# Inverse roots of the two recurrent mixers by one GpSimd power, in a two-block network on one Trainium2 core

## Chip, cores and metric

The program runs on one core of a Trainium2 chip. The metric is device time in microseconds (us) of one execution; three runs of the kernel before gave 1481.28 to 1483.36, median 1481.92. All data are float32, and all work from the input `x` to the output is in one launch.

## The reference, cut to what matters

The network has a first block of two attention layers and a second block of two layers, each `FFN, mixer, FFN`, with 256 tokens of width 1024. The change touches the mixer only. Its recurrent half (eight heads of 64) and its retention half (four heads of 128) are:

```python
kk = heads(k * k_k)
kk = kk * lax.rsqrt(jnp.maximum(jnp.sum(kk * kk, axis=-1, keepdims=True), 1e-24))
...
y = rwkv7_scan(r_h, heads(decay), k_h, v_h, -kk, kk * a_h)
mean = jnp.mean(y, axis=-1, keepdims=True)
var = jnp.mean(jnp.square(y - mean), axis=-1, keepdims=True)
y = ((y - mean) * lax.rsqrt(var + LN_X_EPS) * ln_w + ln_b)
...
o = retention_chunkwise(q, k, v)
o = o * lax.rsqrt(jnp.mean(o * o, axis=-1, keepdims=True) + NORM_EPS)
```

Three inverse roots per head and token, then: of the keys, of the recurrence's output, and of the retention's output. The mixer also has low-rank products (`w_lora_up`, `a_lora_up`) that make the decay and the factor `a`.

## The kernel before

Activations are kept transposed: 128 partitions of features, 256 tokens along the free axis. A weight tile comes from HBM (`raw`, four buffers), is split by ScalarE into a rounded high part (`whi`, line 115) and by VectorE into the rest (`wlo`, line 116), and each product is three matmuls (lines 129 to 131). `fetch_to` runs these loads four tiles ahead of their use.

In `mix` the eight recurrent heads are worked on in two units `b` of four. For each unit: `project` makes k, r and v (`proj_t`, then `shifted`, whose tile `pz` has two buffers in a ring); `operands` takes the norm of the keys; `chunks` makes the Gram matrices of four chunks of 64 tokens (`gram`, line 980) and inverts a triangular matrix by five doubling steps (tiles `t` and `dx`, line 963); `chain` runs the recurrence over the chunks and normalises its output. Then come `retention` and the output product. The functions are generators; the order in which an engine gets their instructions is chosen by a scheduler when the program is built, and each engine runs its own list strictly in that order. So the projections of unit 1 (`mm`) stand in TensorE's list between the small matmuls of unit 0.

One norm goes this way. `by_head` sums squares on TensorE into a PSUM tile `sums` (line 900), 128 tokens by 8 values. `rsqrt` (line 165) takes the inverse root on VectorE in twelve instructions: one for scale and offset, or for the floor (`ra`, line 172 or 174), two for a first guess by integer arithmetic (lines 175 and 176), and three Newton steps of three (lines 178 to 180). `spread2` (line 884) copies the eight values out to 64 columns each on ScalarE (`wide`, line 887, in the ring of `pz`) and transposes that on TensorE (`spread`, line 891), so that the factor stands beside the features. In `operands` a further matmul sums the bonus (`bonus`, line 945). The retention's root (line 1220) goes to TensorE without `wide`.

`lora_pair` (line 867) makes the low-rank products `pw` and `pa` and takes them through ScalarE as `sw` and `av`. For unit 1 it uses the PSUM banks of the projections (tag `mm`, line 1121).

Of the kernel before, what the change touches and what calls it, by code (L numbers as in the profile page):

```python
# [9 lines left out]
F32 = mybir.dt.float32  # L10
# [3 lines left out]
OP = mybir.AluOpType  # L14
# [37 lines left out]
class Net:  # L52
# [3 lines left out]
    def __init__(self, ctx, tc, plan, wstream, x, vec, vcols, ident):  # L56
        self.tc, self.nc = tc, tc.nc
        nc = self.nc
        self.wstream, self.plan = wstream, plan
        self.offs = {}  # L60
        off = 0
        for key, n in plan:
            self.offs[key] = (off, n)
            off += 128 * n
        self.order = [k for k, _ in plan]
        self.pos = {k: i for i, k in enumerate(self.order)}
        self.keep = ctx.enter_context(tc.tile_pool(name="keep", bufs=1))
        self.ring = ctx.enter_context(tc.tile_pool(name="ring", bufs=1))
        self.banks = Banks(ctx.enter_context(tc.tile_pool(name="banks", bufs=1, space=bass.MemoryType.PSUM)))
        xs = [self.keep.tile([128, 2, S], F32, name=f"x{i}") for i in range(4)]  # L70
        self.xs = xs
        self.x = [xs[k // 2][:, k % 2] for k in range(KT)]
        self.gain0 = self.keep.tile([128, KT], F32, name="gain0")
        self.vec = self.keep.tile([128, vec.shape[1]], F32, name="vec")
        nc.sync.dma_start(xs[0], x[:, 0:2])
        nc.scalar.dma_start(self.gain0, vec[:, vcols["norm0"]:vcols["norm0"] + KT])
        self.vcols = vcols
        self.ones = self.keep.tile([128, 128], F32, name="ones")
        nc.gpsimd.memset(self.ones, 1.0)
        self.ident = self.keep.tile([128, 128], F32, name="ident")  # L80
        nc.gpsimd.dma_start(self.ident, ident)
        self.ready = {}
        self.y = {}
        self.next = 0
        self.loads = {}
        self.between = lambda: None

        for i in range(1, 4):
            self.fetch_to(LEAD[i - 1])
            nc.sync.dma_start(xs[i], x[:, 2 * i:2 * i + 2])  # L90
        self.fetch_to(LEAD[3])
        nc.sync.dma_start(self.vec, vec)
# [68 lines left out]
            nc.scalar.activation(t, self.xs[i], AF.Square)  # L161
            nc.vector.tensor_tensor(sq, sq, t, op=OP.add)

    def rsqrt(self, src, shape, scale, eps, name, floor=None):

        nc = self.nc
        full = {"k": [128, 16], "q": [128, 2, 4], "m": [128, 2]}[name]
        a, y, t = (self.ring.tile(full, F32, tag=i + name, name=i, bufs=2)[..., :shape[-1]]
                   for i in ("ra", "ry", "rt"))
        v = nc.vector  # L170
        if floor is None:
            v.tensor_scalar(a, src, scale, eps, op0=OP.mult, op1=OP.add)
        else:
            v.tensor_scalar(a, src, floor, None, op0=OP.max)
        v.tensor_scalar(y.bitcast(I32), a.bitcast(I32), 1, None, op0=OP.logical_shift_right)
        v.tensor_scalar(y.bitcast(I32), y.bitcast(I32), -1.0, float(0x5f3759df), op0=OP.mult, op1=OP.add)
        for _ in range(3):
            v.tensor_tensor(t, y, y, op=OP.mult)
            v.scalar_tensor_tensor(t, t, -0.5, a, op0=OP.mult, op1=OP.mult)
            v.scalar_tensor_tensor(y, t, 1.5, y, op0=OP.add, op1=OP.mult)  # L180
        return y
# [642 lines left out]
    def mix(self, tag, l, cst):  # L824


        nc, tc, ident = self.nc, self.tc, self.ident
# [3 lines left out]
        with ExitStack() as c:  # L831
# [49 lines left out]
                    nc.scalar.activation(t, t, AF.Copy, scale=0.5, bias=0.5)  # L881
                q.update(sw=sw, av=av)

            def spread2(rn, tag):

                wide = work.tile([128, 2, 4, 64], F32, tag="pz", name="wide", bufs=2)
                nc.scalar.copy(wide, rn[:, :, :, None].to_broadcast([128, 2, 4, 64]))
                ps = psum.tile([128, 2, S], F32, tag=tag, name="spread")
                for u in range(2):
                    for tt in range(2):  # L890
                        nc.tensor.transpose(ps[:, u, tt * 128:tt * 128 + 128],
                                            wide[:, tt, 2 * u:2 * u + 2].rearrange("p e d -> p (e d)"), ident)
                return ps
# [19 lines left out]
            def operands(q, b):  # L913

                k, r, v, s_, a = (q[n] for n in ("k", "r", "v", "sw", "av"))
                ls, em = two("op1", "lsem")
                kk, kq = two("op2", "kkq")
                for u in range(2):
                    nc.vector.tensor_tensor_scan(ls[:, u], scan, s_[:, u], 0.0, op0=OP.mult, op1=OP.add)

                e1 = work.tile([128, 8, C + 1], F32, tag="e1", name="e1")
                nc.gpsimd.memset(e1[:, :, 0:1], 1.0)
                nc.scalar.activation(e1[:, :, 1:], c8(ls), AF.Exp, scale=DK)
                ec = work.tile([128, 2, 4], F32, tag="ec", name="ec", bufs=2)
                nc.scalar.copy(ec, e1[:, :, C].rearrange("p (u c) -> p u c", u=2))
                nc.scalar.activation(em, ls, AF.Exp, scale=-DK)
                for u in range(2):
                    nc.scalar.activation(kk[:, u], k[:, u], AF.Copy, scale=self.v(f"kk{l}", 2 * b + u))
                nc.scalar.activation(kq, kk, AF.Square)
                yield  # L930
                rn = self.rsqrt(by_head(kq, "inv"), [128, 2, 4], 1.0, 0.0, "q", floor=1e-24)
                kh = work.tile([128, 2, S], F32, tag="kh", name="kh")
                for u in range(2):
                    nc.scalar.activation(kh[:, u], a[:, u], AF.Identity, scale=self.v(f"ka{l}", 2 * b + u),
                                         bias=rest[:, 14 + 2 * b + u:15 + 2 * b + u])
                nc.vector.tensor_tensor(kh, kh, k, op=OP.mult)

                for u in range(2):
                    nc.vector.scalar_tensor_tensor(kq[:, u], r[:, u], self.v(f"rk{l}", 2 * b + u), kh[:, u],
                                                   op0=OP.mult, op1=OP.mult)  # L940
                yield
                sp = spread2(rn, "inv")
                nc.vector.tensor_tensor(kk, kk, sp, op=OP.mult)
                ps = psum.tile([128, 2, S], F32, tag="inv", name="bonus")
                nc.tensor.matmul(ps, blk, kq, start=True, stop=True)

                ar, bk = w8("ar", 128), w8("bk", 128)
                nc.vector.scalar_tensor_tensor(ar[:, :, 0:64], c8(kk), -1.0, e1[:, :, 0:C], op0=OP.mult, op1=OP.mult)
                nc.vector.tensor_tensor(a, kk, a, op=OP.mult)
                nc.vector.tensor_tensor(bk[:, :, 0:64], c8(a), c8(em), op=OP.mult)  # L950
                nc.vector.tensor_tensor(bk[:, :, 64:128], c8(kh), c8(em), op=OP.mult)
                nc.vector.tensor_tensor(ar[:, :, 64:128], c8(r), e1[:, :, 1:], op=OP.mult)
                bonus = work.tile([128, 2, S], F32, tag="bonus", name="bonus", bufs=2)
                nc.vector.tensor_tensor(bonus, ps, v, op=OP.mult)
                for u in range(2):
                    nc.scalar.activation(bonus[:, u], bonus[:, u], AF.Identity, bias=self.v(f"lb{l}", 2 * b + u))
                q.update(ec=ec, bonus=bonus, ar=ar, bk=bk)
# [77 lines left out]
            def chain(q, b):  # L1035
# [55 lines left out]
                y2 = w8("t1", 64, 1).rearrange("p (u c) t -> p u (c t)", u=2)  # L1091
                nc.scalar.activation(y2, y, AF.Square)
                yield
                rn = self.rsqrt(by_head(y2, "ch"), [128, 2, 4], 1.0 / 64, 64e-5, "q")
                yield
                sp = spread2(rn, "ch")
                nc.vector.tensor_tensor(y, y, sp, op=OP.mult)
                for u in range(2):
                    nc.vector.scalar_tensor_tensor(y[:, u], y[:, u], self.v(f"lw{l}", 2 * b + u), q["bonus"][:, u],
# [16 lines left out]
            def project(name, b):  # L1116
                q = units[b]
                mid = None
                if name == "v":
                    if b:  # L1120
                        lora_pair(q, 1, "mm")
                    else:
                        mid = lambda: lora_pair(q, 0, "inv")
                ps = led["kr".index(name) + 1] if b == 0 and name in "kr" else self.proj_t(psum, (tag, name, b), mid=mid)
                q[name] = work.tile([128, 2, S], F32, tag="p" + name, name="p" + name, bufs=2 if name == "v" else 1)
                shifted(ps, q[name], {"r": 0, "k": 4, "v": 8}[name] + 2 * b)
# [14 lines left out]
    def retention(self, tag, l, psum, work, cst, units):  # L1141
# [75 lines left out]
            if h:  # L1217
                norms(h - 1, sq[h - 1])
        norms(3, sq[3])
        rn = self.rsqrt(ps2, [128, 2, 4], 1.0 / 128, 1e-6, "q")  # L1220
        for h in range(4):
            sp = self.spread(psum, lambda tt: rn[:, tt, h:h + 1].to_broadcast([128, 128]))
            nc.vector.tensor_tensor(o[h], o[h], sp, op=OP.mult)
# [282 lines left out]
```

## Time and profile before

| | value |
|---|---|
| profiled execution, its own time | 1481.24 us |
| its span, first to last instruction | 1479.4 us |
| median of three runs | 1481.92 us |
| TensorE busy (matmuls) | 1442.0 us, 97% |
| VectorE busy | 1027.2 us, 69% |
| ScalarE busy | 739.7 us, 50% |
| GpSimd busy | 6.3 us in 43 instructions |
| mean granted TensorE clock | 0.988 |

TensorE is busy nearly all the time, in 1442.0 of 1479.4 us, so what can be won lies in its holes and in the stretches where its granted clock is below 1. Clock 1.00 means 2.4 GHz and 0.50 means 1.2 GHz. The two mixers begin near 522 us and 1097 us.

### The profile page before, as it was taken

The page shows a single profiled execution, that of the slowest core. Times are in us where ns is not written, and L with a number is a line of the kernel's source. Part 1 is how long each engine was busy: PE and PEld are TensorE (multiplying, and loading weights), DVE is VectorE, ACT ScalarE, POOL GpSimd, SP SyncE. Part 2 cuts the span into 40 slices and gives each one's busy share as a digit, 9 for nine tenths or more (in the row PEclk, how much of TensorE's full clock was granted, in tenths as well). Part 3 has the DMA queues.
Part 4 walks back from the last instruction along what each step waited for, and adds up shares of the span by engine and source line. Part 5 has one row for each costly group of instructions (what it writes and reads, how often), then busy time and mean ns, then how long its engine had stood idle before and what let it go on. Part 6 is the DMA issues. An engine that isn't in the chain of part 4 may idle for free.

```text
span 1479.4 us, 31824 instructions
## 1 busy us (share of the span) xinstructions
PE 1442.0 (97%) x13326; PEld 1379.1 (93%) x13326; DVE 1027.2 (69%) x1914; ACT 739.7 (50%) x1268; POOL 6.3 (0%) x43
## 2 busy tenths in 40 slices
PE   8899989999999989999999999999998999999997
PEld 7799979899999988899999999999997889999997
DVE  7879788976565676768655558556577757865564
ACT  6947555855444574235544445444466314554443
POOL 0000000000000000000000000000000000000000
PEclk9999999999999998999999999999999999999998
DMA  8234534265555541124555555555552213555561
GB/s 291 79 129 143 174 121 136 86 219 174 185 185 184 161 165 64 50 84 139 173 186 182 182 181 176 180 184 186 185 172 86 73 45 101 169 177 183 185 185 44
DMA packets 63601, 222.01 MB, mean 150 GB/s; under 512 B 7745, under 2 KB 9025, under 8 KB 63457
## 3 DMA queue, kind: packets, MB, share of 16 engines
q1 hardware_dynamic: 62928, 219.31, 46.3%
q8 instruction: 104, 1.70, 0.5%
q10 hardware_dynamic: 432, 0.53, 0.1%
q14 instruction: 41, 0.33, 0.1%
q0 software_dynamic: 96, 0.13, 0.0%
HBM read 218.90 MB, written 1.05 MB: 149 GB/s over the span
## 4 chain that ended last, share of the span: by engine, by line
PE 89%; DVE 4%; ACT 4%; issue 1%; DMA 1%; SPq 0%; DVEq 0%; ACTq 0%
PE gu L129 11%; PE gu L130 11%; PE gu L131 11%; PE mm L130 6%; PE mm L129 6%; PE acc L129 6%; PE acc L130 6%; PE acc L131 6%; PE mm L131 6%; PE dx L963 1%; DVE wlo L116 1%; ACT whi L115 1%; PE t L963 1%; PE gu L271 1%; PE gram L980 1%
## 5 line engine op out<-in xcount | busy, mean ns | idle before, releaser
L115 ACT CAST whi<-raw 128x1024 fp32r<-128x1024 f32 (+1 forms) x412 | 426.6, 1038 | 441.7 <-PE gu L130 161.4
L116 DVE TENSOR_TENSOR wlo<-raw,whi 128x1024 fp32r<-128x1024 f32 (+1 forms) x412 | 499.4, 1213 | 205.6 <-ACT whi L115 205.1
L129 PE MATMUL gu<-hh,whi 128*128 128x256 f32 x1344 | 381.2, 284 | 0.0
L130 PE MATMUL gu<-hl,whi 128*128 128x256 f32 x1344 | 380.7, 283 | 0.0
L131 PE MATMUL gu<-hh,wlo 128*128 128x256 f32 x1344 | 380.5, 283 | 0.0
L129 PEld LDWEIGHTS gu<-hh,whi 128*128 128x128 f32 x1344 | 258.0, 192 | 0.6 <-issue 0.4
L130 PEld LDWEIGHTS gu<-hl,whi 128*128 128x128 f32 x1344 | 258.1, 192 | 0.0
L131 PEld LDWEIGHTS gu<-hh,wlo 128*128 128x128 f32 x1344 | 258.0, 192 | 0.0
L131 PE MATMUL acc<-mh,wlo 128*128 128x256 f32 x704 | 198.8, 283 | 0.0
L130 PE MATMUL acc<-ml,whi 128*128 128x256 f32 x704 | 198.8, 283 | 0.0
L129 PE MATMUL acc<-mh,whi 128*128 128x256 f32 x704 | 197.7, 284 | 0.1
L129 PE MATMUL mm<-hh,whi 128*128 128x256 f32 x608 | 180.4, 297 | 8.8 <-ACT whi L115 6.7
L130 PE MATMUL mm<-hl,whi 128*128 128x256 f32 x608 | 177.1, 291 | 0.1
L131 PE MATMUL mm<-hh,wlo 128*128 128x256 f32 x608 | 175.6, 289 | 0.0
L130 PEld LDWEIGHTS acc<-ml,whi 128*128 128x128 f32 x704 | 135.2, 192 | 0.0
L131 PEld LDWEIGHTS acc<-mh,wlo 128*128 128x128 f32 x704 | 135.2, 192 | 0.0
L129 PEld LDWEIGHTS acc<-mh,whi 128*128 128x128 f32 x704 | 134.3, 192 | 0.8 <-issue 0.4
L129 PEld LDWEIGHTS mm<-hh,whi 128*128 128x128 f32 x608 | 117.8, 194 | 15.4 <-ACT whi L115 6.7
L130 PEld LDWEIGHTS mm<-hl,whi 128*128 128x128 f32 x608 | 117.8, 194 | 3.7 <-issue 2.0
L131 PEld LDWEIGHTS mm<-hh,wlo 128*128 128x128 f32 x608 | 117.9, 194 | 1.2 <-DVE wlo L116 0.2
L246 DVE TENSOR_TENSOR t<-gu,rs 128x512 f32<-128x512 f32 x88 | 60.5, 691 | 55.1 <-PE gu L131 55.1
L137 ACT CAST mh<-g 128x256 fp32r<-128x256 f32 x88 | 35.4, 406 | 100.6 <-DVE g L249 100.6
(392 smaller groups left out, 2205.9 us busy)
## 6 DMA issues: line engine op xcount, KB each, us to landing
raw<-in_stream SPq DMA_DIRECT2D x404, 512.0 KB, 3.5
raw<-in_stream SPq DMA_DIRECT2D x4, 280.0 KB, 2.7
x<-in_x SPq DMA_DIRECT2D x4, 256.0 KB, 5.1
raw<-in_stream SPq DMA_DIRECT2D x4, 256.0 KB, 5.3
lora<-in_lora SPq DMA_DIRECT2D x2, 512.0 KB, 6.1
dec<-in_dec SPq DMA_DIRECT2D x1, 512.0 KB, 5.5
out<-o SPq DMA_DIRECT2D x2, 256.0 KB, 3.0
out<-o ACTq DMA_DIRECT2D x2, 256.0 KB, 2.9
```

The costliest lines, as they stand in the source:

```text
L115: nc.scalar.copy(hi, raw)
L116: nc.vector.tensor_tensor(lo, raw, hi.bitcast(F32), op=OP.subtract)
L129: mm(out, ah, bh, start=start, stop=False, skip_group_check=True)
L130: mm(out, ah, bl, start=False, stop=False, skip_group_check=True)
L131: mm(out, al, bh, start=False, stop=stop, skip_group_check=True)
L137: nc.scalar.copy(hi, src)
L246: nc.vector.tensor_tensor(t, ps, self.rsb, op=OP.mult)
L271: mm(ps[:, u], part, self.h[k][0], start=(i + j == 0), stop=False, skip_group_check=True)
L963: nc.tensor.matmul(ps[p, n], lhs(e, p, n), rhs(e, p, n), start=True, stop=True)
L980: nc.tensor.matmul(ps[p, n], bk[p, 4 * u + n, w], ar[p, 4 * u + n], start=True, stop=True)
```

## The change

A new `power` takes the place of `rsqrt` at three places: the keys' norm, the recurrence's norm, and the retention's norm. It has one VectorE instruction for scale or floor (`rp`) and one GpSimd `tensor_tensor` that raises it to the power -0.5 (`rr`). The first block and the RMS norms go on with `rsqrt`. `wide` moves from the ring of `pz` to the two tiles that otherwise hold the squares (`sqt` for unit 0, `sqa` for unit 1). The second `lora_pair` writes to the banks `ch` of the recurrence in place of `mm`.

```diff
+        self.mhalf = self.keep.tile([128, 2, 4], F32, name="mhalf")
+        nc.gpsimd.memset(self.mhalf, -0.5)
...
+    def power(self, src, scale, eps, floor=None):
+
+        nc = self.nc
+        n = src.shape[-1]
+        a, y = (self.ring.tile([128, 2, 4], F32, tag=i, name=i, bufs=2)[..., :n] for i in ("rp", "rr"))
+        if floor is None:
+            nc.vector.tensor_scalar(a, src, scale, eps, op0=OP.mult, op1=OP.add)
+        else:
+            nc.vector.tensor_scalar(a, src, floor, None, op0=OP.max)
+        nc.gpsimd.tensor_tensor(y, a, self.mhalf[..., :n], op=OP.pow)
+        return y
...
-            def spread2(rn, tag):
-
-                wide = work.tile([128, 2, 4, 64], F32, tag="pz", name="wide", bufs=2)
+            def spread2(rn, b, tag):
+
+
+                wide = self.ring.tile([128, 2, 4, 64], F32, tag=("sqt", "sqa")[b], name="wide")
...
-                rn = self.rsqrt(by_head(kq, "inv"), [128, 2, 4], 1.0, 0.0, "q", floor=1e-24)
+                rn = self.power(by_head(kq, "inv"), None, None, floor=1e-24)
...
-                sp = spread2(rn, "inv")
+                sp = spread2(rn, b, "inv")
...
-                rn = self.rsqrt(by_head(y2, "ch"), [128, 2, 4], 1.0 / 64, 64e-5, "q")
+                rn = self.power(by_head(y2, "ch"), 1.0 / 64, 64e-5)
                 yield
-                sp = spread2(rn, "ch")
+                sp = spread2(rn, b, "ch")
...
-                        lora_pair(q, 1, "mm")
+                        lora_pair(q, 1, "ch")
...
-        rn = self.rsqrt(ps2, [128, 2, 4], 1.0 / 128, 1e-6, "q")
+        rn = self.power(ps2, 1.0 / 128, 1e-6)
```

The scheduler builds another order from this. The first place is VectorE's list in the first mixer, from the keys' sums of unit 0 to the factor's use. Before, from the ninth of the twelve root instructions on, the end of the second Newton step (names: `kkq` holds the keys and their squares, `bonus` the bonus sums, `pz` and `pk` the shifted projection of unit 1):

```order
L180 SCALAR_TENSOR_TENSOR ry<-rt,ry 128x8
L116 TENSOR_TENSOR wlo<-raw,whi 128x1024
L178 TENSOR_TENSOR rt<-ry 128x8
L116 TENSOR_TENSOR wlo<-raw,whi 128x1024
L179 SCALAR_TENSOR_TENSOR rt<-rt,ra 128x8
L116 TENSOR_TENSOR wlo<-raw,whi 128x1024
L180 SCALAR_TENSOR_TENSOR ry<-rt,ry 128x8
L852 TENSOR_TENSOR pz<-mm,rs 128x2x256
L943 TENSOR_TENSOR kkq<-kkq,spread 128x512
```

Of the change, from the sums on:

```order
L174 TENSOR_SCALAR rp<-sums 128x8
L948 TENSOR_TENSOR kh<-kh,pk 128x512
L863 TENSOR_TENSOR pz<-mm,rs 128x2x256
L951 SCALAR_TENSOR_TENSOR kkq<-pr,vec,kh 128x256 x2
L963 TENSOR_TENSOR bk<-kh,lsem 128x8x64
L955 TENSOR_TENSOR kkq<-kkq,spread 128x512
L966 TENSOR_TENSOR bonus<-bonus,pv 128x512
L960 SCALAR_TENSOR_TENSOR ar<-kkq,e_6789 128x8x64
L961 TENSOR_TENSOR av<-kkq,av 128x512
L118 TENSOR_TENSOR wlo<-raw,whi 128x1024
L962 TENSOR_TENSOR bk<-av,lsem 128x8x64
```

Five weight splits stood between the root's steps, three of them in the rows shown; now the first split stands behind the factor's use in `kkq`.

The second place is TensorE's list at the same point. Before, 18 projection matmuls lie between `sums` and `bonus` and 33 more between `bonus` and `spread`; of them only the last ones are shown:

```order
L129 MATMUL mm<-hh_6445,whi 128x256
L130 MATMUL mm<-hl_6446,whi 128x256
L131 MATMUL mm<-hh_6445,wlo 128x256
L891 MATMUL spread<-ident,wide 128x128 x4
L874 MATMUL pw<-wag,lora 128x256 x2
L129 MATMUL mm<-hh_6417,whi 128x256
L980 MATMUL gram<-ar,bk 64x128 x8
```

Of the change, 16 lie between `sums` and `spread`, 2 between `spread` and `bonus`, and 14 between `bonus` and the first `gram`:

```order
L131 MATMUL mm<-hh_6435,whi 128x256
L903 MATMUL spread<-ident,wide 128x128 x4
L132 MATMUL mm<-hl_6436,whi 128x256
L133 MATMUL mm<-hh_6435,wlo 128x256
L957 MATMUL bonus<-kkq,blk_108 128x512
```

`spread` thus moves 35 projection matmuls forward. The pairs `pw` and `pa` stand together behind the Gram matrices; before, `pw` stood right behind `spread`. From `sums` to the first `t` matmuls TensorE's list has 81 projection matmuls before and 77 now. The same holds in the second mixer.

## Rows read from the trace of the kernel before

**Rows 1.** Waits of TensorE: line, releaser, us in total, times, longest us.
```profile
PE spread L891 <- ACT wide L887: 6.7, 2, 3.4
PE mm L129 <- ACT sw L878: 1.9, 2, 0.9
```
**Rows 2.** Timeline of TensorE, both mixers: start, us, instruction, count, [idle before <- releaser].
```profile
542.49 1.05 PE L900 MATMUL sums<-e,kkq 128*128 128x2 f32 x8 [0.52 <-ACT kkq L929]
554.05 1.12 PE L891 MATMUL spread<-ident,wide 128*128 128x128 f32 x4 [3.32 <-ACT wide L887]
558.10 0.58 PE L129 MATMUL mm<-hh,whi 128*128 128x256 f32 x1 [0.93 <-ACT sw L878]
570.00 1.15 PE L963 MATMUL t<-x,gb 64*64 64x64 f32 x32
1116.80 1.05 PE L900 MATMUL sums<-e,kkq 128*128 128x2 f32 x8 [0.53 <-ACT kkq L929]
1143.51 1.15 PE L963 MATMUL t<-x,gb 64*64 64x64 f32 x32
```
**Rows 3.** Windows: length, busy us (x) of PE, PEld, DVE, ACT, POOL, PEclk, DMA, GB/s.
```profile
554.00:556.00 2.00, 1.95 (x6) 1.53 (x7) 0.80 (x2) 0.91 (x2) 0.10 (x1) 0.50 0.80 305
564.00:566.00 2.00, 2.00 (x25) 1.60 (x23) 2.00 (x5) 0.00 (x0) 0.00 (x0) 1.00 0.04 8
...
680.00:1100.00 420.00, 419.42 (x3485) 417.95 (x3485) 273.70 (x396) 197.23 (x274) 0.86 (x7) 1.00 0.57 179
```
**Rows 4.** Timelines of VectorE, then ScalarE, at the keys' norm of unit 0.
```profile
543.58 0.17 DVE L174 TENSOR_SCALAR ra<-sums 128x8 f32<-128x8 f32 x1 [2.47 <-PE sums L900]
552.04 1.22 DVE L116 TENSOR_TENSOR wlo<-raw,whi 128x1024 fp32r<-128x1024 f32 x1 [0.22 <-ACT whi L115]
553.18 0.16 DVE L180 SCALAR_TENSOR_TENSOR ry<-rt,ry 128x8 f32<-128x8 f32 x1
553.26 0.68 DVE L852 TENSOR_TENSOR pz<-mm,rs 128x512 f32<-128x512 f32 x1
...
550.96 1.04 ACT L115 CAST whi<-raw 128x1024 fp32r<-128x1024 f32 x1 [1.34 <-DMA raw<-in_stream]
553.38 0.62 ACT L887 COPY wide<-ry 128x512 f32<-128x512 f32 x1 [1.37 <-DVE ry L180]
```
**Rows 5.** Timeline of TensorE at clock 1.00, for the price of each piece.
```profile
565.45 1.13 PE L875 MATMUL pa<-wag,lora 64*128 64x256 f32 x4
567.45 0.60 PE L997 MATMUL vt<-ident,pv 128*128 128x128 f32 x4
596.87 1.02 PE L945 MATMUL bonus<-kkq,blk 128*128 128x512 f32 x2
599.81 0.66 PE L891 MATMUL spread<-ident,wide 128*128 128x128 f32 x4
602.04 1.09 PE L980 MATMUL gram<-ar,bk 64*64 64x128 f32 x16
```
**Rows 6.** Groups by form on GpSimd: busy us, mean ns | idle before <- releasers.
```profile
L840 POOL TENSOR_SCALAR half<-vec 128x4 f32<-128x4 f32 x4 | 0.8, 223 | 898.0 <-DVE x L231 898.0
L419 POOL TENSOR_TENSOR eye<-ident 128x64 f32<-128x64 f32 x1 | 0.3, 317 | 2.5 <-DMA ident<-in_ident 2.5
```
**Rows 7.** Timeline of TensorE and VectorE at the retention's norm, first mixer.
```profile
679.91 0.36 PE L129 MATMUL mm<-yh,whi 128*128 128x256 f32 x1
680.09 0.17 DVE L172 TENSOR_SCALAR ra<-rss 128x8 f32<-128x8 f32 x1 [2.04 <-PE rss L1208]
682.61 0.40 PE L188 MATMUL spread<-ident,ry 128*128 128x128 f32 x2 [0.20 <-DVE ry L180]
```
**Rows 8.** Timeline of VectorE, then TensorE, at two later norms, first mixer.
```profile
594.53 0.16 DVE L174 TENSOR_SCALAR ra<-sums 128x8 f32<-128x8 f32 x1
650.25 0.17 DVE L172 TENSOR_SCALAR ra<-sums 128x8 f32<-128x8 f32 x1 [0.95 <-PE sums L900]
...
651.90 0.36 PE L307 MATMUL mm<-wlo,hh 128*128 128x256 f32 x1
```

More of the change, by code (lines that the diff above doesn't have):

```diff
@@ L162, in squares, with rsqrt @@
             nc.vector.tensor_tensor(sq, sq, t, op=OP.add)
-    def rsqrt(self, src, shape, scale, eps, name, floor=None):
+    def power(self, src, scale, eps, floor=None):
[8 more added lines that the diff above has]
+        return y
+    def rsqrt(self, src, shape, scale, eps, name):
         nc = self.nc
@@ L170, in rsqrt @@
         v = nc.vector
[L171 to L174, printed above, removed]
+        v.tensor_scalar(a, src, scale, eps, op0=OP.mult, op1=OP.add)
         v.tensor_scalar(y.bitcast(I32), a.bitcast(I32), 1, None, op0=OP.logical_shift_right)
```

## The prediction

> **What bounds the kernel.** I read the page's busy shares first (TensorE 1442.0 of 1479.4 us), then the waits of TensorE, to see where its remaining holes are. Inside the mixers two waits stand out, each once per mixer: the transposition `spread` waits for ScalarE's `wide`, 6.7 us together, and a projection waits for `sw`, 1.9 us together [rows 1]. The timeline places them: `spread` starts at 554.05 after 3.32 us of nothing, the projection at 558.10 after 0.93 us [rows 2]. The windows show what such a hole also does. The granted clock is 0.50 at 554 to 556 us and back at 1.00 at 564 to 566 [rows 3]; the engine had been idle for 3.32 us before it fell, and TensorE works at 1.2 GHz for several us behind the hole.
>
> Why `wide` is late is in the other two timelines. The sums are in VectorE's hands at 543.58, but the last step of the twelve comes at 553.18, 9.6 us later, for 12 steps of about 0.17 us [rows 4]. The scheduler had put weight splits (`wlo`) between the steps. One of them, at 552.04, waits for a ScalarE cast, which at 550.96 had itself waited 1.34 us for a weight transfer [rows 4]. So a step of 0.16 us stands in a queue behind work that nobody on this path needs.
>
> **The change, part by part.** My sum covers the stretch from the keys' `sums` of unit 0 to the first `t` matmuls, since TensorE's list holds the same pieces there before and now, but for four projection matmuls. Before, it takes 570.00 - 542.49 = 27.5 us in the first mixer and 1143.51 - 1116.80 = 26.7 us in the second [rows 2].
>
> TensorE's own work there at clock 1.00: 77 projection matmuls by 419.42 / 3485 = 0.120 us [rows 3] are 9.3 us. `sums` take 1.05 [rows 2]; `spread` 0.66, `bonus` 1.02, four Gram groups by 1.09, two low-rank groups by 1.13 and `vt` 0.60 [rows 5] are 8.9. Together 19.2 us, and 0.5 us for the four matmuls that now come later make 19.7. If no wait is left, the stretch gives back 7.8 us in the first mixer and 7.0 in the second, 14.8 us. That is the holes of rows 1 plus what the half clock cost. Everything behind it moves up, as TensorE is full from there on.
>
> Does the new path fit under what TensorE has to do? It gets 16 matmuls between `sums` and `spread` (1.9 us), so it is free for `spread` about 2.9 us after 542.49, near 545.3. On the other side `rp` takes VectorE from 543.58 to 543.75. Then comes the power on GpSimd, with a duration p that no row shows, then `wide`, 0.62 us [rows 4], and three hand-offs of 0.05 to 0.1 us. `spread` can start at 544.6 + p, so up to **p = 0.7 us** the path is hidden. In GpSimd's list the power stands behind memsets of `pz`; the last of these needs only reads that VectorE's list has ahead of `rp`, so they are done.
>
> The price p: the nearest rows are GpSimd's 128x4 instruction, 0.22 us, and its 128x64 one, 0.32 us [rows 6]. The lower bound is the first, 0.22. The slope is (317 - 223) / 60 = 1.6 ns for each element and step. A power of 8 elements made of some 40 elementary steps would add 8 x 40 x 1.6 ns = 0.5 us. As upper bound I take all twelve steps of the old root at GpSimd's small price, 12 x 0.223 = 2.7 us. My value is 0.7, near the lower row because it is one instruction on very few elements. That is an estimate from these rows.
>
> Cover at the later norms, counted the same way:
> - Unit 1's keys: `rp` can start at about 594.53 [rows 8], and TensorE has 13 matmuls, a small group and `bonus` ahead of `spread`; hidden up to p = 1.3.
> - The recurrence's norms: `rp` at 650.25, and TensorE reaches the end of the second sums at 651.90 [rows 8], with only three matmuls (29 before) up to `spread`; hidden up to p = 1.05.
> - The retention: TensorE resumes matmuls at 679.91 and `ra` starts at 680.09 [rows 7]. The list leaves four matmuls there (19 before), 0.5 us. With p = 0.7 and 0.2 us of hand-offs `spread` starts at 681.15, a hole of 0.75 us where 0.20 was [rows 7]: 0.55 us lost per mixer, **1.1 us** in all.
>
> Removed VectorE steps (55 per mixer) give VectorE time, which pays only where TensorE waits for it: zero. `wide` in the squares' tiles costs nothing, since these are idle until the next FFN's squares. `lora_pair` in the banks of the recurrence takes away the wait for `sw`, already in the sum; those banks are next wanted by the recurrence, some 20 us later.
>
> Two small terms are taken against each other. Neighbouring pieces overlap at their ends, so 19.2 us is up to about 0.8 too long per mixer. Against that, VectorE's list is now dense and `t` and `dx` will wait a few tenths several times; I put 1.0 us per mixer. Net 0.4 lost.
>
> The sum: 14.8 - 1.1 - 0.4 = 13.3 us. Against the profiled execution's 1481.24 us (0.68 below the median of 1481.92) this is 1467.9, given as **1468.0 us**. 0.2% is 3.0 us, about what a measurement of this kernel can tell from no change.
>
> **Rivals.**
> 1. *The power is longer than its cover* (p from 1.05 to 2.6). Each us beyond the cover is a hole at four places per mixer. At p = 2.0 the extra is 1.3 + 0.7 + 0.95 + 1.3 = 4.25 us per mixer, 8.5 in all: 1476.5. For it: no power has run here. Against: 8 values per partition. Chance 0.13.
> 2. *Slower: the power dearer than what it replaces.* If GpSimd goes through it element by element, p passes 2.6 and the four new holes per mixer exceed the 7.4 us given back; from there it is slower. At p = 4: 3.3 + 2.7 + 2.95 + 3.3 = 12.25 per mixer, 24.5 in all, 1492.5, and more if the clock falls. For it: the scheduler has planned for a short power and left three or four matmuls of cover. Against: 4 us would be some 300 steps per element at rows 6. Chance 0.10.
> 3. *VectorE becomes the bound.* From `rp` to the transposition ahead of `t` its list has 4 splits by 1.22 us, 16 wide instructions by 0.68, 4 half-wide by about 0.47 and `rp`: 17.8 us [rows 4], from 543.58 to 561.4, while TensorE arrives at 542.5 + 19.2 = 561.7. There is no slack: a wait on a cast such as that of 1.34 us shifts `t`. At 2 us per mixer: 1472. Chance 0.10.
> 4. *The first power is dear, the others are not.* A load of the power's code before its first use would open a hole at the first mixer's `spread` alone; if it eats that mixer's 7.8 us, 1475.8. Rows 6 show GpSimd's first `tensor_tensor` at 0.317 us in all, without one. Chance 0.05. The Trainium skill (GPSIMD Engine Reference, section 2.1, Instruction dispatch) says that the first call of a freshly loaded routine costs about 6 us more, unseen by the profile; by that the sum would be some 5 to 8 us less in gain, and no row here shows such a load.
>
> That the change does not shorten the path at all is excluded by the list: `spread` stands 35 matmuls earlier.
>
> **How the numbers follow.** Forecast 0.62, rivals 0.13, 0.10, 0.10, 0.05. The forecast's own span runs from 1464.6 (no small waits, p at its lower bound) to about 1471. Rivals 3, 4 and most of 1 end by 1480, so the range is **1464.5 to 1480.0**; the upper bound p = 2.7, which gives 1482, lies outside with rival 2. Faster by over 0.2% (below 1478.3): the forecast, 3, 4 and p up to 2.2 of rival 1, together 0.86. Same: the rest of rival 1 and the edge of 2, 0.05. Slower: 0.09.
>
> **What would show it.** Right: no wait of `spread` on `wide` over 0.3 us, granted clock 1.00 through both mixers, stretches from `sums` to `t` of 19 to 21 us, a POOL row of about 0.7 us ten times, a hole of about 0.8 us at each retention norm. Wrong: a power over 1.3 us, with holes at `spread` in all four kinds of place (rivals 1 and 2); `t` waiting for VectorE's `x` (rival 3); the first power alone late (rival 4).

## The result, and the profile after

The changed kernel takes 1467.18 us (median of 4 runs, 1466.96 to 1471.22) against 1481.6 us before (4 runs, 1480.47 to 1483.36): ratio 0.9908, 95% interval 0.9888 to 0.9928. The profiled execution took 1467.17 us, 14.07 us less than the one shown before; its span is 1465.4 us. TensorE is busy in 1432.1 us of it, GpSimd in 23.9 us in place of 6.3.

The waits of TensorE after (line, releaser, us in total, times, longest us), to hold against [rows 1]:

```profile
PE spread L199 <- POOL rr L175: 3.1, 2, 1.5
PE spread L903 <- ACT wide L899: 2.8, 4, 1.0
```

The wait of `spread` on `wide` is down from 6.7 to 2.8 us, the wait for `sw` is gone, and there is a new one: the retention's `spread` waits for the power itself, 1.5 us in each mixer. The timeline of TensorE answers to [rows 2, 7, 8]:

```profile
541.25 1.05 PE L912 MATMUL sums<-e,kkq 128*128 128x2 f32 x8 [0.52 <-ACT kkq L941]
...
545.34 0.66 PE L903 MATMUL spread<-ident,wide 128*128 128x128 f32 x4 [1.02 <-ACT wide L899]
...
560.43 1.15 PE L975 MATMUL t<-x,gb 64*64 64x64 f32 x32 [0.16 <-DVE x L1000]
...
589.54 0.60 PE L903 MATMUL spread<-ident,wide 128*128 128x128 f32 x4
...
643.30 1.11 PE L903 MATMUL spread<-ident,wide 128*128 128x128 f32 x4 [0.40 <-ACT wide L899]
...
674.29 0.43 PE L199 MATMUL spread<-ident,rr 128*128 128x128 f32 x2 [1.53 <-POOL rr L175]
...
1109.00 1.05 PE L912 MATMUL sums<-e,kkq 128*128 128x2 f32 x8 [0.53 <-ACT kkq L941]
...
1128.17 1.15 PE L975 MATMUL t<-x,gb 64*64 64x64 f32 x32 [0.16 <-DVE x L1000]
```

From `sums` to the first `t` it is now 19.18 and 19.17 us, where it was 27.51 and 26.71. The granted clock is 1.00 there. In the mixers it falls once, as the small hole in front of 643.30 opens, and is at 0.50 for some 3.4 us; at the same hole of the second mixer it stays at 1.00. The windows after (columns as in [rows 3]):

```profile
554.00:556.00 2.00, 2.00 (x26) 1.69 (x24) 1.79 (x4) 1.41 (x4) 0.10 (x1) 1.00 0.65 254
...
642.50:643.00 0.50, 0.40 (x3) 0.18 (x2) 0.17 (x1) 0.37 (x1) 0.24 (x2) 0.96 0.00 0
...
644.00:646.00 2.00, 2.00 (x11) 2.00 (x11) 1.48 (x2) 1.30 (x4) 0.49 (x1) 0.50 0.00 0
```

GpSimd's timeline gives the price of the power, which no row before could give. The four kinds of place in the first mixer, in order of time:

```profile
542.59 2.04 POOL L175 TENSOR_TENSOR rr<-rp,mhalf 128x8 f32<-128x8 f32 x1 [2.49 <-DVE rp L174]
...
586.90 1.81 POOL L175 TENSOR_TENSOR rr<-rp,mhalf 128x8 f32<-128x8 f32 x1 [31.98 <-DVE rp L174]
640.96 1.64 POOL L175 TENSOR_TENSOR rr<-rp,mhalf 128x8 f32<-128x8 f32 x1 [52.25 <-DVE rp L172]
642.85 1.64 POOL L175 TENSOR_TENSOR rr<-rp,mhalf 128x8 f32<-128x8 f32 x1 [0.26 <-DVE rp L172]
672.60 1.64 POOL L175 TENSOR_TENSOR rr<-rp,mhalf 128x8 f32<-128x8 f32 x1 [28.11 <-DVE rp L172]
```

**Where the 14.07 us come from.** The first RMS norm's `spread` of each FFN and of each mixer is a landmark in both traces. Between landmarks, a mixer took 189.72 and 188.90 us before and takes 184.60 and 183.77 now: 10.25 us less. The four FFN stretches took 192.39, 192.34, 192.24 and 182.00 us and now take 191.67, 191.57, 191.55 and 181.32: another 2.86 us, in code that the diff does not touch. One pair of these rows, TensorE, before:

```profile
716.42 0.40 PE L188 MATMUL spread<-ident,ry 128*128 128x128 f32 x2
...
908.76 0.40 PE L188 MATMUL spread<-ident,ry 128*128 128x128 f32 x2 [0.19 <-DVE ry L180]
```

and after:

```profile
710.07 0.40 PE L199 MATMUL spread<-ident,ry 128*128 128x128 f32 x2
...
901.64 0.41 PE L199 MATMUL spread<-ident,ry 128*128 128x128 f32 x2 [0.19 <-DVE ry L191]
```

The rest, some 0.9 us, lies ahead of the first landmark (0.5) and behind the last (0.4).

Two questions follow. Is it the power that frees the mixer? And what made the FFNs shorter?

### The profile page after: what moved, and what is told of

Its sections match the earlier page's. It is cut to its first block, busy times and chain, and to the rows that moved or that the text cites. A ratio compares the mean times of both kernels' runs of the same rounds, so it can differ in the third digit from the quotient of the medians.

```text
span 1465.4 us, 31747 instructions
## 1 busy us (share of the span) xinstructions
PE 1432.1 (98%) x13326; PEld 1370.9 (94%) x13326; DVE 1013.0 (69%) x1804; ACT 739.8 (50%) x1268; POOL 23.9 (2%) x54
## 3 DMA queue, kind: packets, MB, share of 16 engines
HBM read 218.90 MB, written 1.05 MB: 150 GB/s over the span
## 4 chain that ended last, share of the span: by engine, by line
PE 91%; ACT 4%; DVE 3%; issue 1%; POOL 1%; DMA 0%; POOLq 0%; DVEq 0%; ACTq 0%
PE gu L131 11%; PE gu L133 11%; PE gu L132 11%; PE mm L132 6%; PE mm L131 6%; PE mm L133 6%; PE acc L131 6%; PE acc L132 6%; PE acc L133 6%; PE t L975 2%; PE dx L975 1%; PE gram L992 1%; PE gu L282 1%; PE s L370 1%; ACT whi L117 1%
```

## Experiments: what frees the mixer

All times below are medians of the runs made beside the kernel before, which took 1481.0 to 1481.4 us there.

**The old root at all three norms, the two moved buffers kept.**

```diff
-                rn = self.power(by_head(kq, "inv"), None, None, floor=1e-24)
+                rn = self.rsqrt(by_head(kq, "inv"), [128, 2, 4], 1.0, 0.0, "q", floor=1e-24)
...
-                rn = self.power(by_head(y2, "ch"), 1.0 / 64, 64e-5)
+                rn = self.rsqrt(by_head(y2, "ch"), [128, 2, 4], 1.0 / 64, 64e-5, "q")
...
-        rn = self.power(ps2, 1.0 / 128, 1e-6)
+        rn = self.rsqrt(ps2, [128, 2, 4], 1.0 / 128, 1e-6, "q")
```

> The change with the old root of twelve steps at all three norms: only the tile of wide and the banks of the second low-rank pair stay changed. Theory (the single power lets spread stand early; the tiles alone do not): 1476 to 1478 us, that is the layout's 2.9 us and the 1.9 us of the waits for sw, with a wait of spread on wide of 2 to 3.5 us per mixer still there. Rival (the two moved buffers set the order free and made the gain): 1467 to 1469, no such wait.

Measured: 1467.85 us, ratio 0.9912 (0.9898 to 0.9925). The rival holds. Without a single power the kernel is as fast as the change. In the mixers it is even faster: they take 182.59 and 182.64 us, 13.4 us less than before in all, where the change wins 10.25; the change's total also holds the 2.86 us of the FFNs, which this run does not have. TensorE reaches `spread` with no hole in front:

```profile
541.79 1.05 PE L915 MATMUL sums<-e,kkq 128*128 128x2 f32 x8 [0.53 <-ACT kkq L944]
...
551.04 0.66 PE L906 MATMUL spread<-ident,wide 128*128 128x128 f32 x4
```

**Only `wide` moved, from the kernel before.**

```diff
-                wide = work.tile([128, 2, 4, 64], F32, tag="pz", name="wide", bufs=2)
+                wide = self.ring.tile([128, 2, 4, 64], F32, tag=("sqt", "sqa")[b], name="wide")
```

> The kernel before with wide moved out of the ring of pz, nothing else: no power, banks as before. Theory (the ring held the shift of unit 1's projection, and with it the projections, until the root was done; the tile alone frees them): 1468 to 1471 us, no wait of spread on wide over 0.3 us, the wait for sw still there or a part of it. Rival (the banks of the second low-rank pair made the gain of the run with the old root): 1477 us or more, the wait of 3.3 us still there.

Measured: 1470.88 us, ratio 0.9928 (0.9915 to 0.994); no wait of `spread` on `wide`, and 0.3 us left of each wait for `sw`. The theory holds. VectorE's timeline of this run shows what the ring did:

```profile
543.80 0.17 DVE L174 TENSOR_SCALAR ra<-sums 128x8 f32<-128x8 f32 x1 [2.47 <-PE sums L900]
...
544.76 0.68 DVE L852 TENSOR_TENSOR pz<-mm,rs 128x512 f32<-128x512 f32 x1
...
551.03 0.16 DVE L180 SCALAR_TENSOR_TENSOR ry<-rt,ry 128x8 f32<-128x8 f32 x1
```

The projection of unit 1 is taken out of PSUM into `pz` at 544.76, 1 us after VectorE has the sums. Before, that `pz` stands at 553.26, right behind the last root step [rows 4]. That fits a ring whose turns are given out in the program's order: `wide` comes ahead of this `pz`, so `pz` was placed only once the root was (read from the lists; the run shows that the ring is what matters). Unit 1's shift stood still meanwhile, and the scheduler filled VectorE's list with weight splits. Five splits stood between the root's steps then, two do in this run, and the last step starts 7.2 us after the first, not 9.6.

**Only the banks moved, from the kernel before.**

```diff
-                        lora_pair(q, 1, "mm")
+                        lora_pair(q, 1, "ch")
```

> The kernel before with the second low-rank pair in the banks of the recurrence, nothing else. Theory (these banks only take away the wait for sw and put 1.1 us of work ahead of spread; the ring of pz still blocks): 1477 to 1479.5 us, a wait of spread on wide of 2 us or more in each mixer. Rival (the banks alone free the order): 1472 us or less.

Measured: 1472.97 us, ratio 0.9946 (0.9933 to 0.9958). The theory was right that the waits on `wide` stay and wrong on the size: 8.4 us are won, not 2 to 4. TensorE's timeline and the windows of this run show part of why:

```profile
554.30 0.66 PE L891 MATMUL spread<-ident,wide 128*128 128x128 f32 x4 [2.33 <-ACT wide L887]
...
1123.31 1.11 PE L891 MATMUL spread<-ident,wide 128*128 128x128 f32 x4 [2.47 <-ACT wide L887]
```

```profile
554.00:556.00 2.00, 1.70 (x15) 1.70 (x16) 1.20 (x3) 2.00 (x5) 0.10 (x1) 1.00 1.02 334
...
1124.00:1126.00 2.00, 2.00 (x11) 2.00 (x11) 1.54 (x3) 1.97 (x5) 0.10 (x1) 0.50 0.89 307
```

At the 2.33 us hole of the first mixer the granted clock stays at 1.00; at the 2.47 us hole of the second it falls to 0.50, for some 3.4 us. Before, with holes of 3.32 and 3.40 us, it was at 0.50 for some 10 and 7 us. Counted over a whole mixer in steps of 1 us, the idle time of TensorE and the time lost to the clock (busy time by one less the granted clock) are:

| run | mixer 0: length, idle, lost to clock | mixer 1: length, idle, lost to clock |
|---|---|---|
| before | 189.7, 5.4, 3.9 | 188.9, 5.5, 3.0 |
| only banks moved | 184.3, 4.8, 0 | 185.7, 4.9, 1.5 |
| only `wide` moved | 183.4, 2.8, 0 | 184.9, 2.8, 1.7 |
| both, old root | 182.6, 2.5, 0 | 182.6, 2.5, 0 |
| the change | 184.6, 4.0, 1.6 | 183.8, 4.2, 0 |
| power at keys only | 181.4, 2.2, 0 | 181.4, 2.2, 0 |
| power twice | 198.8, 11.4, 9.0 | 197.2, 11.5, 7.0 |

Of the 8.6 us that the banks win in the two mixers, 5.4 are clock and 1.2 idle time. What is left when both are taken off differs by up to 2.3 us between rows; that the other order makes neighbouring pieces overlap differently is likely, but was not split further.

**The change with `wide` back in the ring of `pz`.** (The diff is that of the second experiment turned round, in the changed kernel.)

> The change with wide put back into the ring of pz: the power at all three norms and the moved banks stay. Theory (a short root and a moved tile are two ways out of the same block, each enough): 1467 to 1470 us. Rival (the ring blocks with any root): 1473 us or more, with a wait of spread or a hole behind it of 2 us or more per mixer.

Measured: 1467.03 us, ratio 0.9905 (0.9892 to 0.9919). The theory holds: with the short root the ring costs nothing, though it still orders. Unit 1's `pz` stands late on VectorE here too:

```profile
551.98 0.68 DVE L863 TENSOR_TENSOR pz<-mm,rs 128x512 f32<-128x512 f32 x1
```

That is the pattern of all the runs looked at: with `wide` in the ring this `pz` stands behind the root (553.26 before, 553.52 with the banks moved, 551.98 here), with `wide` moved it stands within 1 us of the first step on the sums. So the moved tile and the moved banks are two remedies for one block, each enough for most of the gain, and beside the moved banks the short root does about what the moved tile does. The short root with neither buffer moved was not run, so what it wins alone is open. The gains do not add: 10.1 us for the tile alone, 8.4 for the banks alone, 13.2 for both. With the power on top the total is 14, but 2.9 of that are the FFNs' (next part but one); in the mixers the power on top takes the gain down, from 13.4 us to 10.25, or 11.6 in the run here.

## Experiments: what the power costs

**The power at the keys' norm alone**, the second and third pair of lines of the first diff above applied to the change.

> The change with the old root at the recurrence's and at the retention's norm, the power at the keys' norm alone. Theory (the power pays at the keys' norm and costs 1.3 us per mixer at the retention and 0.4 us and some clock at the recurrence): 1463.0 to 1464.5 us, retention's wait back at 0.2 us, recurrence's at none. Rival (the power pays there too, since VectorE is relieved of 33 small steps per mixer): 1467 to 1469.

Measured: 1462.49 us, ratio 0.9875 (0.986 to 0.989), 4.7 us under the change and a little below what was expected. TensorE's list is that of the change up to the recurrence's norm. Its waits on roots in this run:

```profile
PE spread L202 <- DVE ry L194: 3.5, 6, 2.5
PE spread L906 <- ACT wide L902: 2.0, 2, 1.0
```

The mixers take 181.43 and 181.41 us, 1.2 us each less than with the old root and the same two buffers moved: that is what the power at the keys is worth. The retention waits 0.20 us again, the recurrence not at all; what is left on `wide` are the two holes of 1.0 us at the keys of unit 0. At the other norms the old root had enough matmuls beside it (29 and 19) and the power, short in the scheduler's plan, was given three and four.

**The power twice.**

```diff
+        nc.gpsimd.tensor_tensor(y, y, self.ones[:, 0:2 * n].rearrange("p (a b) -> p a b", a=2), op=OP.pow)
```

> The change with a second GpSimd power (exponent 1) behind each first one, so the price p per root is doubled, some 1.7 us more, at all ten places. Theory (beyond its cover the power's time is a hole of TensorE one for one): per mixer about 2.0 at the keys of unit 0, 1.5 at those of unit 1, 1.6 and 1.6 at the recurrence's, 1.6 at the retention's: 8.3, in all 16 to 18 us, 1483 to 1485. Rival (the roots still lie mostly beside other work, or what waits behind spread waits for VectorE anyway): under 8 us more, below 1475.

Measured: 1495.25 us, ratio 1.0095 (1.0081 to 1.0109), 28 us above the change and 10 above what was expected. The waits:

```profile
PE spread L904 <- ACT wide L900: 14.6, 6, 3.0
...
PE spread L200 <- POOL rr L176: 6.3, 2, 3.1
```

Together 20.9 us, where the change has 5.9: the holes grow by 15.0, near the 16 to 18 expected. What was left out is the clock: 16 us are lost to it in the two mixers, against 1.6. Taken together, the holes of this run cost about twice their length.

**The price by the number of values**, measured beside the last FFN.

```diff
+    for r in range(6):
+        for i, (w, op) in enumerate(((1, OP.pow), (2, OP.pow), (8, OP.pow), (8, OP.pow), (16, OP.pow), (32, OP.pow),
+                                     (8, OP.mult), (32, OP.mult))):
...
+            g.tensor_tensor(y[:, 0:w], b[:, 0:w], e[:, 0:w], op=op)
```

> The change, and beside the last FFN, where GpSimd has nothing to do, 48 more tensor_tensor on it of 128 rows: powers of 1, 2, 8, 16 and 32 values, products of 8 and 32. Nobody reads their results. Theory (the price goes with the number of values in a row): 8 values 1.64 us as in the change, 1 value about 0.3, 32 values 6 to 7 us; products of 8 and 32 some 0.2 and 0.3 us. Rival (the price is that of the call): 1 value 1.3 us or more, 32 values under 2.5. Beside a busy VectorE both get longer, up to 2.5 us for 8 values. The added tiles put mh 512 bytes further from the weights than in the kernel before less nothing, so a multiple of 512 again: by the addresses' theory the FFN is back at 192.3 us and the whole at 1470 us; by the rival that any shift helps 1467.

Groups by form on GpSimd in this run (busy us, mean ns); `yp` are powers, `ym` products:

```profile
L1476 POOL TENSOR_TENSOR yp<-b,pe 128x32 f32<-128x32 f32 x6 | 33.3, 5558 | 0.5
L1476 POOL TENSOR_TENSOR yp<-b,pe 128x8 f32<-128x8 f32 x12 | 21.9, 1829 | 0.9
L1476 POOL TENSOR_TENSOR yp<-b,pe 128x16 f32<-128x16 f32 x6 | 18.6, 3106 | 0.5
...
L1476 POOL TENSOR_TENSOR yp<-b,pe 128x1 f32<-128x1 f32 x6 | 4.4, 737 | 0.5
L1476 POOL TENSOR_TENSOR yp<-b,pe 128x2 f32<-128x2 f32 x6 | 4.4, 731 | 0.5
L1476 POOL TENSOR_TENSOR ym<-b,pe 128x8 f32<-128x8 f32 x6 | 2.1, 350 | 0.5
L1476 POOL TENSOR_TENSOR ym<-b,pe 128x32 f32<-128x32 f32 x6 | 1.6, 272 | 0.5
```

The theory holds from 8 values on: (5.558 - 3.106) / 16 = 0.153 us a value, on some 0.6 us. Below that it does not: 1 and 2 values cost 0.73 us alike, where 0.3 was expected for 1. A product of 32 values costs 0.27. The median, 1472.32 us (ratio 0.9942, 0.9928 to 0.9955), is some 2 us above the 1470 expected; the mean granted clock of its executions is 0.989, against 0.991 and 0.992 in those of the change that took 1467 us. Its FFN is back at 192.29 us, which bears on the next part.

## Experiments: why the FFNs got shorter

The page shows it in the weight loads of TensorE. Before, then after (busy us, mean ns):

```profile
L130 PEld LDWEIGHTS gu<-hl,whi 128*128 128x128 f32 x1344 | 258.1, 192 | 0.0
...
L130 PEld LDWEIGHTS acc<-ml,whi 128*128 128x128 f32 x704 | 135.2, 192 | 0.0
```

```profile
L132 PEld LDWEIGHTS gu<-hl,whi 128*128 128x128 f32 x1344 | 257.3, 191 | 0.0
...
L132 PEld LDWEIGHTS acc<-ml,whi 128*128 128x128 f32 x704 | 132.7, 189 | 0.0
```

The loads of the down product (`acc`) went from 192 to 189 ns, those of the gate and up product (`gu`) hardly moved. What the change alters there is only where buffers lie: the new tile `mhalf` and the buffers of `rp` and `rr` push later buffers up.

**All buffers 32 bytes higher.**

```diff
+        self.pad = self.keep.tile([128, 2, 4], F32, name="pad")
+        nc.gpsimd.memset(self.pad, 0.0)
```

> The kernel before with one unused tile of 32 bytes a partition put in front of the buffers, so that every later buffer has its address 32 bytes higher, as in the change (160 for the last pools there); no instruction but one memset is added and the order is that of before. Theory (the 0.7 us that each FFN lost between the two traces, 2.9 us in all, come from the addresses): about 1478.7 us, the FFN from one norm's spread to the next 191.6 us in place of 192.3. Rival (chance, or another chip): 1481.5 us, FFN 192.3. Second rival (the removed steps and the power did it): also 1481.5.

Measured: 1481.11 us, ratio 1.0 (0.9991 to 1.0009), FFN 192.36 us. The theory, tested in this form, falls. But this run moved weights and activations by the same 32 bytes, and left out the 128 bytes of `rp` and `rr`, which lie between them and part them by 128 more.

**The 128 bytes alone, with the old root.**

```diff
+        gap = late.tile([128, 32], F32, name="gap")
+        nc.gpsimd.memset(gap, 0.0)
```

> The run with the old root at all norms (1467.85 us), and one unused tile of 128 bytes a partition ahead of the constants of the second block, so that the FFN's buffers mh and ml get the very addresses that they have in the change; the order is the same. Theory (the address of mh, 160 bytes on, not 32, is what makes an FFN 0.7 us shorter): 1465.0 us, FFN from spread to spread 191.6 us. Rival (it is not the addresses but something that the power brings): 1467.8 us, FFN 192.3.

Measured: 1465.32 us, ratio 0.9894 (0.9879 to 0.9909), against 1467.85 for the same kernel without the gap; the FFN between two landmarks takes 191.64 us. The theory holds: the FFNs' gain has nothing to do with the power. It also shows what the three powers are worth together. With the FFN's buffers placed as in the change, the old root takes 1465.32 us (1464.54 to 1465.72), the change 1467.18, and the change with `wide` in the ring, measured beside this run, 1467.03 (1466.71 to 1467.58): the powers cost 1.7 to 1.9 us.

**128 bytes ahead of `hh` and `hl`, with the power at the keys only.**

```diff
+        gap = self.ring.tile([128, 32], F32, name="gap")
+        nc.gpsimd.memset(gap, 0.0)
```

> The run with the power at the keys' norm alone (1462.49 us), and one unused tile of 128 bytes a partition ahead of the buffers hh and hl; these and all later ones lie 128 bytes higher. Theory (matmuls go a little faster where the moving operand does not lie a multiple of 512 bytes from the weights, as mh in the change): gu matmuls from 0.120 us apart to some 0.1187, FFN below 191 us, 1455 to 1459 us in all. Rival (only mh reacts, or its own address counts): 1462 to 1466 us.

Measured: 1458.22 us, ratio 0.9845 (0.9832 to 0.9859). Now `gu` is quick (188 ns a load) and `acc`, whose buffers now lie 256 bytes further from the weights than in the kernel before, not 128, is slower again (191). A gap of 96 numbers (384 bytes) more ahead of the second block's constants makes that 640, which is 512 and 128, and should then bring both:

> The power at the keys' norm alone, hh and hl 128 bytes higher as in the run before (1458.22 us), and mh and ml 384 bytes more, so that both lie 128 bytes past a multiple of 512 from the weights. Theory (that distance counts, for each pair of buffers by itself): gu weight loads of 188 ns and acc weight loads of 188 to 189 ns in one run, 1455 to 1456 us. Rival (the gain of gu and that of acc come from something they share and exclude each other): 1458 us or more.

Measured: 1455.55 us, ratio 0.9828 (0.9815 to 0.9842), the fastest version. The weight loads, first with the gap at `hh` alone, then with both gaps:

```profile
L134 PEld LDWEIGHTS gu<-hl,whi 128*128 128x128 f32 x1344 | 253.3, 188 | 0.0
...
L134 PEld LDWEIGHTS acc<-ml,whi 128*128 128x128 f32 x704 | 134.7, 191 | 0.0
```

```profile
L134 PEld LDWEIGHTS gu<-hl,whi 128*128 128x128 f32 x1344 | 253.3, 188 | 0.0
...
L134 PEld LDWEIGHTS acc<-ml,whi 128*128 128x128 f32 x704 | 132.7, 188 | 0.0
```

The next table has, for each run, by how many bytes the added tiles move the activations away from the weights `whi`, against the kernel before and less whole multiples of 512. That shift sorts all of them:

| run | `hh` | `mh` | load of `gu`, ns | load of `acc`, ns | FFN, us |
|---|---|---|---|---|---|
| before | 0 | 0 | 192 | 192 | 192.3 |
| all 32 higher | 0 | 0 | 192 | 192 | 192.4 |
| powers beside the FFN | 0 | 0 | 192 | 192 | 192.3 |
| the change | 0 | 128 | 191 | 189 | 191.6 |
| old root, 128 bytes | 0 | 128 | 191 | 189 | 191.6 |
| 128 at `hh` | 128 | 256 | 188 | 191 | 191.0 |
| both 128 | 128 | 128 | 188 | 188 | 190.4 |

The weights themselves were never moved against fixed activations. So whether the distance counts, or the activations' own address in steps larger than the 32 bytes of the first run, is not told apart.

**The same addresses with no power at all.**

> The same addresses of hh, hl, mh and ml, with the old root at all three norms and no GpSimd power at all. Theory (at equal addresses the power at the keys' norm is worth the 2.8 us between the runs of 1462.5 and 1465.3): 1458 to 1459 us. Rival (those 2.8 us were other addresses too): 1455 to 1456.5, level with the run beside it.

Measured: 1458.9 us, ratio 0.9844 (0.983 to 0.9857). At equal addresses the power at the keys' norm is worth 3.4 us here, where single executions of the two kernels spread by 2.5 and 3.8 us and overlap, and 2.8 in the pair above (1465.32 less 1462.49), where they do not. The theory holds.

## Why the prediction came out, and which steps did not

The time came within 1 us of 1468.0, but partly through errors that cancel: 13.3 us were to come from the mixers, which gave 10.25; 2.86 more came from the FFNs and some 0.9 from the two ends of the program, for which the sum had no term. By the signs that it set itself the forecast fails: they asked for no wait of `spread` on `wide` over 0.3 us and a power of about 0.7 us, and named a power over 1.3 us, with holes at `spread` in all four kinds of place, as a sign of being wrong. The power takes 1.64 to 2.04 us, and holes of 1.02, 0.40 and 1.53 us stand at three of the four. The time is right, the way to it in large part not. By its own steps:

- **The stretch from `sums` to `t`: right.** 19.7 us was forecast, 19.18 and 19.17 came, even with a hole of 1.02 us that p = 0.7 did not foresee; the pieces overlap by more than the 0.8 us set aside for it. It gave back 15.9 us, not 14.8; the holes at the later norms and a fall of the clock took part of that back.
- **What gives it back: wrong on what is needed.** The short root is a way to it (with `wide` back in the ring and the banks moved, 1467.03), but the sum gave it everything and the moved buffers only the wait for `sw`. The step that failed is "`wide` in the squares' tiles costs nothing, since these are idle". It priced the tile by what its new place costs and did not ask what its old place held up. I read the five splits between the root's steps as the scheduler's choice; they stood there while `wide`, in the ring of `pz`, kept unit 1's shift waiting for the root; with the tile moved two are left. Moving the tile alone wins 10.1 us. That the banks take away "the wait for `sw`" only was the second half of the error: alone they win 8.4.
- **The price p = 0.7: too low.** The power takes 1.64 us with VectorE idle and up to 2.04 beside it. The step that failed is the slope of 1.6 ns for each element and elementary step, from two instructions that are not powers; the measured slope is 153 ns a value, where 40 steps, a number that no row gives, made 64. The upper bound, 2.7, stood.
- **The cover: counted somewhat too small.** At the measured p the covers of 0.7, 1.3 and 1.05 us give holes of 1.3, 0.5 and 0.6 us, and the retention one of 1.7; 1.02, none, 0.40 and 1.53 came. So rival 1's condition came true (p within 1.05 to 2.6), but not its 1476.5.
- **The retention: right in kind.** A loss of 0.55 us a mixer was forecast and 1.33 came (1.53 less 0.20). At the recurrence none was forecast; 0.4 us a mixer came. The two make 3.5 us of the 4.7 that the run with the power at the keys alone gains; the rest was not split. The 1.6 us lost to the clock in the first mixer are not needed for it: the second mixer, with no fall, is 2.4 us longer than with the power at the keys alone.
- **The FFNs: missing.** No term stood for buffers that shift, and 2.9 us came from it; the view that only TensorE's holes and its clock leave something to win had no place for it. Without it the change would have been at about 1470; the run with 48 instructions beside the last FFN, whose FFNs are back at 192.3 us, took 1472.32 with more falls of the clock.
- **The other rivals.** VectorE as the bound: `t` waits 0.16 us for `x`, no more. A dear first power: the first one starts 0.25 us after its `rp` begins and takes 2.04 us, as the first of the second mixer does; no load of code shows. Slower than before: at twice the price, 3.3 to 4.4 us a root, the kernel takes 1495.25, so the mechanism was real, and it decides between one and two powers.
- **Two readings.** The clock did not fall behind 3.32 us of nothing. The window 552.5 to 553 below shows it falling inside the hole, some 1.9 us after TensorE's last matmul; in the second mixer it fell 1 us after the matmuls had come back. And rival 2's holes have to eat 13.3 / 2 = 6.65 us a mixer, which is what p = 2.6 gives, not the 7.4 named there.

```profile
552.50:553.00 0.50, 0.00 (x0) 0.00 (x0) 0.50 (x1) 0.00 (x0) 0.00 (x0) 0.60 0.99 401
```

Chance had a part: with the measured p and the rest of the sum as it was, the four places cost 1.3 + 0.5 + 0.6 + 0.9 = 3.3 us more per mixer, and the forecast would have been about 1474.6.

## What to carry to other kernels

Before pricing a step by the steps that it removes, look for what the scheduler could not place: a tile that shares a ring with another unit's work makes that unit wait for whatever fills the tile, and filler work between short steps is the sign of it. Where a new instruction is short in the plan but has no row, count its cover at every place it goes to, and keep the old form where there was cover enough. Compare stretches that the diff does not touch, too: if they moved, look at the addresses before crediting the change. And an engine that is busy nearly all the time can still get faster: with the old root, an FFN went from 192.4 to 190.4 us by added tiles alone.

## What the runs showed of the hardware

- A GpSimd power of 128 rows costs, from 8 values in a row on, some 0.6 us and 0.153 us for each value; 1 and 2 values cost 0.73 us; a product of 8 or 32 values 0.27 to 0.35 us.
- A power of 8 values took 2.04 us beside a busy VectorE and 1.64 beside an idle one. VectorE's timeline in the change, beside the first power (542.59 to 544.63):

```profile
542.42 0.68 DVE L948 TENSOR_TENSOR kh<-kh,pk 128x512 f32<-128x512 f32 x1
543.02 0.68 DVE L863 TENSOR_TENSOR pz<-mm,rs 128x512 f32<-128x512 f32 x1
543.62 0.87 DVE L951 SCALAR_TENSOR_TENSOR kkq<-pr,vec,kh 128x256 f32<-128x256 f32 x2
544.41 0.69 DVE L963 TENSOR_TENSOR bk<-kh,lsem 128x512 f32<-128x512 f32 x1
```

  The Trainium skill (SBUF — State Buffer, section SBUF: two separate sides) says that a GpSimd operation that reads SBUF and a VectorE one with two SBUF inputs shut each other out for the whole instruction. Here the two `kkq` instructions, with two such inputs each, ran wholly inside the power, at their usual 0.48 us apiece, and `bk` started in it at 544.41 and took its usual 0.69 us: the trace does not show VectorE held up, only the power longer. Whether the power's 0.40 us more are a wait for `kh`, which also has two such inputs, had started first and ended at 543.10, no run tells.
- A weight load of 128x128 took 192 ns with the moving operand placed as in the kernel before, and 192 again with it 512 bytes further from the weights in the partition; it took 191 at 256 bytes further and 188 to 189 at 128 or 640. No other shift against the weights was tried, and why it is so stays open. Over all FFNs it is worth 2.9 us for `acc`; shifting `hh` and `hl` as well brought the keys-only version from 1462.49 to 1455.55.
- The clock does not answer to a hole alone. In the run of the old root with 128 bytes, the second mixer's clock is at 0.50 at 1216 to 1218 us, with no hole in front; in the run without them, with the same order, it is 1.00 at the same place in the program, 3 us later. First with the 128 bytes, then without:

```profile
1216.00:1218.00 2.00, 2.00 (x11) 2.00 (x11) 2.00 (x14) 0.00 (x0) 0.00 (x0) 0.50 0.27 51
```

```profile
1218.00:1220.00 2.00, 2.00 (x19) 2.00 (x19) 2.00 (x7) 0.36 (x1) 0.00 (x0) 1.00 0.00 0
```

  Falls of this kind cost 1.5 to 1.7 us each. Single executions of one kernel differ by 1 to 4 us, and the clock can be a part of that: the change's execution of 1471.22 us had a mean clock of 0.989, the three near 1467 had 0.991 and 0.992.
